# A hybrid decoder layer on one core: retention's state sums in the bank of pv, its normalisation on ScalarE, and the first half of w_out split by casting and adding DMAs

## The chip, the cores and the metric

One of the eight cores of a Trainium2 chip runs the kernel; the others stand idle. The metric is the device time of one execution in microseconds (us); lower is better. The kernel before was timed three times, and one more execution was profiled.

## The reference, cut to what matters

One decoder layer over 512 tokens of width 1024, all in float32:

```
h    = rms_norm(x);  proj = h @ w_in                    # columns split among the head groups
mix  = concat[retention(rq, rk, rv, rg), nsa(...)] @ w_out
x    = x + rms_norm(mix)
x    = x + rms_norm(conv_ffn(rms_norm(x)))
```

Retention has 4 heads and works in chunks of 128 tokens. For each chunk and head:

```
scores  = (q @ k.T) * decay                  # 128 x 128, causal
o       = scores @ v + (q @ state) * xi      # state: 64 x 128, from the chunks before
state   = state * gamma**128 + (k * zeta).T @ v
o       = (o - mean(o)) * rsqrt(var(o) + 1e-5)   # over the 128 columns of the head
y_ret   = silu(g) * (o * gn_w)
```

`mix` is the product of `concat[y_ret, y_nsa]` (512 x 1024) with `w_out` (1024 x 1024).

## The kernel before, in words

Every float32 product is made of three passes over float32r parts: a matrix is split into a high part (`wh`, `xh`, `yh`) and a low part (`wl`, `xl`, `yl`), and `mm3` multiplies high by high, high by low and low by high. So each weight has to be split before TensorE (PE) can take it. There are two ways. `nextw` (through `loadw` and `splitw`) loads the raw weight with a DMA of SyncE (SP), copies it to `wh` on ScalarE (ACT) and subtracts on VectorE (DVE). `castw` lets GpSimd's (POOL's) DMA queue do it:

```
loaded[0] = pool.dma_start(wh, src)                  # casts to float32r while it copies
copy(wl, f(wh), scale=-1.0)                          # on ScalarE
pool.dma_start(wl, src, accum_op=ALU.add)            # adds the source to -wh
```

A class `_Plan` records all operations with a rank, and then sets the order of every engine by itself (`schedule`): it plays the kernel through with its own table of costs, and gives each engine, among the operations that could start within 20 ns of the first, the one of lowest rank. The engines then run their lists in order. The order is fixed at build time. Tiles come from pools by tag, each tag with a number of buffers; a tile takes the next free buffer of its tag in the order in which the program names the tiles.

The stretch that the change touches lies between the attention branches (rank 10) and the output projection (rank 20):

- `ret_a(t)`, for the chunks t = 0 to 3 (rank 5, so ahead of all else): scores `rs` on PE, the mask `sT` on DVE, the output `ro` on PE (with the state `ST` for t > 0), the state's sums `kv` on PE, `ST` brought up to date on DVE, mean and variance of `ro` on DVE (`bs`, `mv`), the reciprocal root `rs` on POOL (a power, and a product with `xi`), and the normalised output into `RV` on DVE. `rs`, `ro` and `kv` are PSUM banks of the tag `m` (`mps`), which has three; the attention's `pv` has a tag of its own with one bank (`pvps`).
- The projection `w_rg` (a `Chunk` of rank 17.8, split by `castw`) gives the gate: `G` and `th` on ACT from four banks `acc`, then products on DVE. Its matmuls (`acc<-wh,xh` and so on, 128x512) stand on PE between those of attention and retention wherever the planner found a gap.
- `ret_b(t)` multiplies `G` by `RV`, transposes it on PE (`tp<-cn,G`, four 128x128 each) and splits it into `yh`, `yl`.
- `c0`, the `Chunk` for the first 512 columns of `w_out` (rank 20): its four weight parts are `wo`, split by `nextw`; parts 0 and 1 take the attention's half of y, parts 2 and 3 retention's. The second 512 columns (`wo1`, banks named `wo`) and the feed-forward follow.

Before a part of rank 0 or 20 is split, line 595 asks `if 0 < plan.rank < 20` for `castw`. All instructions carry line 398, the emitter's, so groups are told apart by tiles.

Of the kernel before, what the change touches and what calls it, by code (L numbers as in the profile page):

```python
# [11 lines left out]
AF = mybir.ActivationFunctionType  # L12
ALU = mybir.AluOpType
AX = mybir.AxisListType

P = 128
# [386 lines left out]
def _body(ctx, tc, io, out, soff, coff):  # L403
# [5 lines left out]
    plan = _Plan(nc)  # L409
    pe, act, dve, pool, sync = (plan.engine(e) for e in (PE, ACT, DVE, POOL, SP))  # L410
# [5 lines left out]
    def nm(s):  # L416
        cnt[0] += 1
        return f"{s}_{cnt[0]}"
# [10 lines left out]
    def k8(shape, dt=F32, n="k"):  # L429
        return plan.tile(gp, shape, dt, nm(n), "k8", 5)  # L430
# [4 lines left out]
    def f2(shape, dt=F32, n="t"):  # L435
        return plan.tile(gp, shape, dt, nm(n), "f2", 6)
# [7 lines left out]
    def tiny(shape, n="y"):  # L444
        return plan.tile(gp, shape, F32, nm(n), "tiny", 16)
# [44 lines left out]
    def castw(src, a, b, wide=False, spare=False):  # L490

        if wide:
            both = k8([P, 2, a, b], F32R, "wb")
            wh, wl = both[:, 0], both[:, 1]
        elif spare:
            wh, wl = (plan.tile(st, [P, a, b], F32R, nm(n), "raw", 2) for n in ("wh", "wl"))
        else:
            wh, wl = (plan.tile(st, [P, a, b], F32R, nm(n), n, 4) for n in ("wh", "wl"))
        loaded[0] = pool.dma_start(wh, src)
        copy(wl, f(wh), scale=-1.0)  # L500
        pool.dma_start(wl, src, accum_op=ALU.add)
        return wh, wl
# [7 lines left out]
    def nextw(src, a, b, eng=dve_pool, **k):  # L510
        return splitw(loadw(src, a, b, **k), eng=eng)
# [35 lines left out]
    def C(name):  # L547
        o, n = coff[name]
        return cn[:, o:o + n]
# [10 lines left out]
    def rsqrt(o, var, n):  # L560
        pool.tensor_tensor(o, var, mhalf[:, :n], op=ALU.pow)
# [21 lines left out]
    def mm3(o, ah, al, bh, bl, start, stop, **k):  # L583
        pe.matmul(o, ah, bh, start=start, stop=False, **k)
        pe.matmul(o, ah, bl, start=False, stop=False, **k)
        pe.matmul(o, al, bh, start=False, stop=stop, **k)

    class Chunk:
# [3 lines left out]
            self.acc = [acc() for _ in range(NT)]  # L592

        def part(self, js, pre=None):
            if 0 < plan.rank < 20 and js[0] >= self.first:
                W = {j: castw(self.src[j], 2, self.n, spare=j == 0) for j in js}
            else:
                W = {j: pre or nextw(self.src[j], 2, self.n, eng=dve if plan.rank else dve_pool) for j in js}
            if 3 in js:
                order = [(j, a, t) for t in range(NT) for j in js for a in range(2)]  # L600
            else:
                order = [(j, a, t) for j in js for a in range(2) for t in range(NT)]
            for j, a, t in order:
                wh, wl = W[j]
                ts = slice(t * P, (t + 1) * P)
                mm3(self.acc[t][:, :self.n], self.lh[j][:, a, ts], self.ll[j][:, a, ts], wh[:, a, :], wl[:, a, :],
                    j == 0 and a == 0, j == 3 and a == 1)
                if j == 3 and a == 1:
                    self.evac(t, self.acc[t])
# [364 lines left out]
    RB = mps  # L974
# [4 lines left out]
    def ret_a(t):  # L979
        rq, rk, rv = RQ[0][:, t], RK[0][:, t], RV[0][:, t, :]  # L980
        m = RB("rs").rearrange("p (h i) -> p h i", h=4)
        for h in range(4):
            pe.matmul(m[:, h, :], rk[:, h // 2, h % 2, :], rq[:, h // 2, :], start=True, stop=True)
        sT = f2([P, 4, P], n="sT")
        dve.tensor_tensor(sT, m, C("rmask").unsqueeze(1).to_broadcast([P, 4, P]), op=ALU.mult)
        o = RB("ro").rearrange("p (h e) -> p h e", h=4)
        for h in range(4):
            pe.matmul(o[:, h, :], sT[:, h, :], rv[:, h * P:(h + 1) * P], start=True, stop=t == 0)
            if t > 0:
                pe.matmul(o[:, h, :], rq[:, h // 2, :], ST[:, h // 2, h % 2, :], start=False, stop=True)  # L990
        if t < 3:
            kvp = RB("kv").rearrange("p (a b e) -> p a b e", a=2, b=2)
            for p in range(2):
                pe.matmul(kvp[:, p].rearrange("p b e -> p (b e)"), RN[0][:, t, p * P:(p + 1) * P],
                          rv[:, 256 * p:256 * p + 256], start=True, stop=True)
            for q in range(2):
                r = slice(64 * q, 64 * q + 64)
                if t > 0:
                    dve.tensor_tensor(ST[r, :, q, :], kvp[r, :, q, :], ST[r, :, q, :], op=ALU.add)
                else:  # L1000
                    dve.tensor_copy(ST[r, :, q, :], kvp[r, :, q, :])
            for p in range(2):
                dve.tensor_scalar(ST[:, p], ST[:, p], gC[:, p:p + 1], None, op0=ALU.mult)
        bs, mv = tiny([P, 4, 6], "bs"), tiny([P, 4, 2], "mv")
        for h in range(4):
            dve.bn_stats(bs[:, h, :], o[:, h, :])
            dve.bn_aggr(mv[:, h, :], bs[:, h, :])
        rs = tiny([P, 4], "rs")
        dve.tensor_tensor(rs, mv[:, :, 1], C("xi2"), op=ALU.mult)
        dve.tensor_scalar(rs, rs, 1e-5, None, op0=ALU.add)  # L1010
        rsqrt(rs, rs, 4)
        pool.tensor_tensor(rs, rs, C("xi"), op=ALU.mult)
        yn = rv.rearrange("p (h e) -> p h e", h=4)
        for h in range(4):
            dve.tensor_scalar(yn[:, h, :], o[:, h, :], mv[:, h, 0:1], rs[:, h:h + 1], op0=ALU.subtract, op1=ALU.mult)

    def ret_b(t):
        ts = slice(t * P, (t + 1) * P)
# [93 lines left out]
    for t in range(NT):  # L1112
        ret_a(t)
# [168 lines left out]
    def prep(a11, a12, s1, s3, w):  # L1282
        s24 = blk(st, "wl", 4, F32)
        b2, b4 = s24[:, 0], s24[:, 1]
        dve.tensor_tensor(b2, s1, a11, op=ALU.subtract)
        for n, src, tag in (("1", a11, "wh"), ("2", a12, "wh"), ("6", b2, "wh"), ("5", s1, "wh"), ("7", s3, "wl"), ("3", b4, "wl")):
            if n == "6":
                dve.tensor_tensor(b4, a12, b2, op=ALU.subtract)
            w[n] = blk(st, tag, 4)
            part(w[n], src)  # L1290
        return w
# [49 lines left out]
    for n, src in (("5", [t13[0]]), ("6", hb[0]), ("7", [t13[1]]), ("4", hb[1])):  # L1341
# [4 lines left out]
        h, l = MV[n]  # L1346
# [104 lines left out]
    for tt in range(2):  # L1451
        b = k8([P, 4, 512], n="base")
# [37 lines left out]
    for j in range(NP):  # L1490
        if j + 2 < NP:
            lasts.append(t_last(j + 2))
        t = plan.tile(st, [P, 2, 512], F32R, nm("t"), ("wh", "wl")[j % 2], 4)
# [59 lines left out]
```

## Time and profile before

| | |
|---|---|
| median of 3 runs | 635.27 us (635.21 to 636.09) |
| the profiled execution | 637.12 us, of which the span from the first to the last instruction is 635.2 us |
| TensorE clock granted, mean | 0.993 of full speed |
| busy share of the span | PE 97%, DVE 86%, ACT 68%, POOL 28% |
| DMA | 100.21 MB, 158 GB/s over the span |

The profile gives busy time for each engine, the waits that ended idle time, and a list of instructions in order of time. An instruction's row has its start, its length, and in brackets the idle time of its engine before it with what released it. A matmul's length overlaps the next one's, so how fast a run of matmuls goes is read from the distance of the starts.

### The profile page before, as it was taken

The numbers are of one execution on the slowest core, as the hardware profiler recorded it, in microseconds if no ns is written. First come the engines' busy times: TensorE is split into PE (matmuls) and PEld (weight loads), VectorE is DVE, ScalarE is ACT, GpSimd is POOL, SyncE is SP. The second block draws the span as 40 slices with busy tenths as digits, with TensorE's granted clock in tenths as the row PEclk, the third lists the DMA queues.
The fourth block names the chain that finished last, engine by engine and source line by source line (L and its number), as shares of the span: only waits on it lengthen the run. The fifth ranks groups of instructions, "written<-read, shape, count | busy, mean of one in ns | idle before, by whom it ended". The sixth has DMA issues, their size and how long they took to land. (4 is left out here: it accounts for less than half of the span.)

```text
span 635.2 us, 10860 instructions
## 1 busy us (share of the span) xinstructions
PE 613.9 (97%) x3781; PEld 542.4 (85%) x3781; DVE 547.1 (86%) x1159; ACT 430.0 (68%) x882; POOL 179.1 (28%) x205
## 2 busy tenths in 40 slices
PE   8998999989999989999999999999999999999996
PEld 5887988878878877889999999999999997787874
DVE  6369876998878899488999998999999999898994
ACT  6667566868997732466867766776777677777761
POOL 0253432433212415024032423233232212231040
PEclk8999999999999999999999999999999999999999
DMA  8762448512412322439359678978967668998452
GB/s 288 267 229 85 151 128 171 133 34 74 94 33 87 114 94 107 162 136 227 80 126 210 141 186 176 201 144 209 196 164 169 150 183 208 224 254 242 140 208 84
DMA packets 41527, 100.21 MB, mean 158 GB/s; under 512 B 4736, under 2 KB 4864, under 8 KB 41472
## 3 DMA queue, kind: packets, MB, share of 16 engines
q0 software_dynamic: 17424, 36.97, 31.0%
q1 hardware_dynamic: 23904, 62.29, 28.4%
q8 instruction: 30, 0.49, 0.3%
q10 hardware_dynamic: 144, 0.26, 0.1%
q14 instruction: 25, 0.20, 0.1%
HBM read 95.30 MB, written 4.19 MB: 157 GB/s over the span
## 5 line engine op out<-in xcount | busy, mean ns | idle before, releaser
L398 POOL DMA_DIRECT2D b<-wup x80 | 63.6, 940 | 152.8 <-ACT b L398 71.9
L398 DVE TENSOR_TENSOR b<-b,b 128x512 fp32r<-128x512 f32 (+1 forms) x160 | 103.8, 683 | 2.7 <-ACT b L398 1.5
L398 ACT ACTIVATE b<-b 128x512 fp32r<-128x512 f32 (+1 forms) x160 | 92.6, 624 | 15.1 <-DMA b<-wup 6.8
L398 PE MATMUL acc<-wl,xh 128*128 128x512 f32 (+1 forms) x192 | 74.5, 388 | 0.2 <-DVE wl L398 0.2
L398 PE MATMUL acc<-wh,xh 128*128 128x512 f32 (+1 forms) x192 | 72.8, 384 | 1.7 <-DVE wh L398 1.7
L398 ACT ACTIVATE wh<-raw 128x1024 fp32r<-128x1024 f32 (+2 forms) x51 | 52.0, 1020 | 32.5 <-PE acc L398 9.4
L398 PE MATMUL acc<-wh,xl 128*128 128x512 f32 (+1 forms) x192 | 73.6, 383 | 0.0
L398 DVE TENSOR_TENSOR wl<-raw,wh 128x1024 fp32r<-128x1024 f32 (+2 forms) x52 | 61.5, 1189 | 7.0 <-ACT wh L398 6.8
L398 PE MATMUL G<-h2h,b 128*128 128x256 f32 x320 | 64.7, 284 | 1.7 <-ACT p L398 1.1
L398 PE MATMUL X<-T,b 128*128 128x256 f32 x480 | 64.9, 284 | 0.6 <-DVE b L398 0.6
L398 PEld LDWEIGHTS X<-T,b 128*128 128x128 f32 x480 | 60.5, 192 | 1.3 <-DVE b L398 1.0
L398 PE MATMUL X<-h2h,b 128*128 128x256 f32 x320 | 61.3, 284 | 0.0
L398 PEld LDWEIGHTS G<-h2h,b 128*128 128x128 f32 x320 | 52.8, 192 | 2.3 <-ACT p L398 1.3
L398 PEld LDWEIGHTS X<-h2h,b 128*128 128x128 f32 x320 | 51.4, 192 | 0.4 <-DVE X L398 0.2
L398 PE MATMUL G<-h2l,b 128*128 128x256 f32 x160 | 45.3, 283 | 0.0
L398 PE MATMUL X<-h2l,b 128*128 128x256 f32 x160 | 45.3, 283 | 0.0
L398 PEld LDWEIGHTS acc<-wh,xh 128*128 128x128 f32 x192 | 36.4, 191 | 7.5 <-ACT xh L398 2.2
L398 PEld LDWEIGHTS acc<-wl,xh 128*128 128x128 f32 x192 | 37.0, 193 | 5.9 <-DVE wl L398 0.7
L398 PEld LDWEIGHTS acc<-wh,xl 128*128 128x128 f32 x192 | 37.0, 193 | 5.4
L398 ACT ACTIVATE P<-P,nmx 128x256 f32<-128x256 f32 (+3 forms) x64 | 35.2, 553 | 4.7 <-DVE nmx L398 4.7
L398 PE MATMUL d<-wl,ah 128*128 128x512 f32 x88 | 34.5, 395 | 0.9 <-DVE wl L398 0.8
L398 PE MATMUL d<-wh,ah 128*128 128x512 f32 x88 | 33.1, 395 | 1.6 <-ACT wh L398 1.6
(291 smaller groups left out, 1640.9 us busy)
## 6 DMA issues: line engine op xcount, KB each, us to landing
b<-wup POOLq DMA_DIRECT2D x80, 256.0 KB, 5.9
b<-wup SPq DMA_DIRECT2D x60, 256.0 KB, 5.8
raw<-wdn SPq DMA_DIRECT2D x19, 512.0 KB, 5.1
T<-wdn POOLq DMA_DIRECT2D x21, 256.0 KB, 5.6
raw<-wo SPq DMA_DIRECT2D x8, 512.0 KB, 3.3
T<-wdn SPq DMA_DIRECT2D x10, 256.0 KB, 5.5
xraw<-xT SPq DMA_DIRECT2D x8, 256.0 KB, 5.4
xnat<-x SPq DMA_DIRECT2D x4, 512.0 KB, 6.2
```

The source lines that it names most:

```text
L398: i = getattr(getattr(self.nc, op.eng), method)(*a, **k)
```

## The change

Three edits. `castw` is also taken at rank 20, so the four weight parts of `c0` are split by POOL's DMAs and ACT rather than by SP's DMAs, ACT and DVE. The state's sums `kv` of chunks 1 and 2 take the bank of `pv` in place of one of the three of `m`. And the normalised output is one ACT instruction per head, `ro * rs + nb`, where DVE makes `nb = -mean * rs` first.

```
-            if 0 < plan.rank < 20 and js[0] >= self.first:
+            if 0 < plan.rank <= 20 and js[0] >= self.first:
                 W = {j: castw(self.src[j], 2, self.n, spare=j == 0) for j in js}
...
-            kvp = RB("kv").rearrange("p (a b e) -> p a b e", a=2, b=2)
+            kvp = (RB if t == 0 else pvps)("kv").rearrange("p (a b e) -> p a b e", a=2, b=2)
...
         yn = rv.rearrange("p (h e) -> p h e", h=4)
+        nb = tiny([P, 4], "nb")
+        dve.scalar_tensor_tensor(nb, mv[:, :, 0], -1.0, rs, op0=ALU.mult, op1=ALU.mult)
         for h in range(4):
-            dve.tensor_scalar(yn[:, h, :], o[:, h, :], mv[:, h, 0:1], rs[:, h:h + 1], op0=ALU.subtract, op1=ALU.mult)
+            act.activation(yn[:, h, :], o[:, h, :], AF.Identity, scale=rs[:, h:h + 1], bias=nb[:, h:h + 1])
```

The planner then sets another order from the end of attention to the first rows of the second half of `w_out`; before and behind that stretch the lists are the same. Numbers of buffers differ between the two builds.

On PE, around the output of chunk 2 (`ro_640` before, `ro_642` now; `acc` with `xh` is the projection `w_rg`). Before:

```order
L398 MATMUL kv_634<-RV_253,RN_254 128x256 x2
L398 MATMUL rs_638<-RQ_251,RK_252 128x128 x4
L398 MATMUL acc_662<-wl_670,xh_127 128x512
L398 MATMUL acc_662<-wh_669,xl_128 128x512
L398 MATMUL acc_662<-wh_669,xh_127 128x512
L398 MATMUL acc_662<-wl_670,xh_127 128x512
L398 MATMUL acc_662<-wh_669,xl_128 128x512
L398 MATMUL ro_640<-RV_253,sT_639 128x128
L398 MATMUL ro_640<-ST_95,RQ_251 128x128
```

Now:

```order
L398 MATMUL kv_635<-RV_253,RN_254 128x256 x2
L398 MATMUL rs_640<-RQ_251,RK_252 128x128 x4
L398 MATMUL acc_664<-wh_673,xh_127 128x512
L398 MATMUL acc_664<-wl_674,xh_127 128x512
L398 MATMUL kv_643<-RV_253,RN_254 128x256 x2
L398 MATMUL acc_664<-wh_673,xl_128 128x512
L398 MATMUL acc_664<-wh_673,xh_127 128x512
L398 MATMUL ro_642<-RV_253,sT_641 128x128
L398 MATMUL ro_642<-ST_95,RQ_251 128x128
```

Before, these were the last five products of `w_rg`; now they are products 7 to 10 of the 24 of its last part, and the state's sums of chunk 2 stand ahead of its output instead of behind it. In all, 15 products of `w_rg`'s last part stood ahead of the first `ro` before, and none stands there now.

On POOL, from the last factors of attention (`cb`) to the reciprocal root of chunk 1 (`rs_637` before, `rs_638` now). Before:

```order
L398 TENSOR_TENSOR cb_572<-ch_570,cn_73 128x512
L398 TENSOR_TENSOR cb_573<-cl_571,cn_73 128x512
L398 TENSOR_TENSOR rs_630<-rs_630,mhalf_69 128x4
L398 TENSOR_TENSOR rs_630<-rs_630,cn_73 128x4
L398 TENSOR_TENSOR rs_637<-rs_637,mhalf_69 128x4
L398 TENSOR_TENSOR rs_637<-rs_637,cn_73 128x4
```

Now:

```order
L398 DMA wh_692<-wo 128x1024
L398 TENSOR_TENSOR cb_572<-ch_570,cn_73 128x512
L398 TENSOR_TENSOR cb_573<-cl_571,cn_73 128x512
L398 DMA wl_693<-wo 128x1024
L398 DMA wh_694<-wo 128x1024
L398 TENSOR_TENSOR rs_630<-rs_630,mhalf_69 128x4
L398 TENSOR_TENSOR rs_630<-rs_630,cn_73 128x4
L398 TENSOR_TENSOR rs_638<-rs_638,mhalf_69 128x4
L398 DMA wl_695<-wo 128x1024
L398 TENSOR_TENSOR rs_638<-rs_638,cn_73 128x4
```

Four of the eight new DMA issues stand among these, one of them between the two steps of chunk 1's reciprocal root; the other four stand earlier, among attention's work.

On ACT, from the last steps of attention to the gate (`G`, `th`). Before:

```order
L398 ACTIVATE wh_691<-raw_690 128x1024
L398 ACTIVATE G_255<-acc_659,hrstd_78 128x512
L398 ACTIVATE G_255<-acc_660,hrstd_78 128x512
L398 ACTIVATE ch_570<-ct_569 128x128
L398 ACTIVATE ph_575<-tp_574 128x512
L398 ACTIVATE pvl_577<-pv_565 64x512
L398 ACTIVATE G_255<-acc_661,hrstd_78 128x512
L398 ACTIVATE yh_653<-y_28_94 128x2x128
L398 ACTIVATE G_255<-acc_662,hrstd_78 128x512
L398 ACTIVATE wh_694<-raw_693 128x1024
L398 ACTIVATE th_671<-acc_659,hrstd_78 128x512
```

Now:

```order
L398 ACTIVATE wl_693<-wh_692 128x1024
L398 ACTIVATE ph_575<-tp_574 128x512
L398 ACTIVATE pvl_577<-pv_565 64x512
L398 ACTIVATE G_255<-acc_663,hrstd_78 128x512
L398 ACTIVATE yh_657<-y_28_94 128x2x128
L398 ACTIVATE RV_253<-ro_626,nb_631,rs_630 128x128 x4
L398 ACTIVATE wl_695<-wh_694 128x1024
L398 ACTIVATE RV_253<-ro_634,nb_639,rs_638 128x128 x4
L398 ACTIVATE G_255<-acc_664,hrstd_78 128x512
L398 ACTIVATE th_675<-acc_663,hrstd_78 128x512
```

The `RV` of chunks 0 and 1 are new here, the copies `wh<-raw` have become `wl<-wh`, and three of the four steps `G` have moved behind them.

## Rows read from the trace of the kernel before

**Rows 1.** The page's first two parts: busy us, share and instructions of each engine over the span, and PE's granted clock in 40 equal slices, in tenths of full speed.
```profile
PE 613.9 (97%) x3781; PEld 542.4 (85%) x3781; DVE 547.1 (86%) x1159; ACT 430.0 (68%) x882; POOL 179.1 (28%) x205
PEclk8999999999999999999999999999999999999999
```
**Rows 2.** Busy time of each engine by stretches (us from the span's start), with granted clock, DMA share and GB/s. Retention runs from 220.87 to about 250.
```profile
core 0: us, PE busy (x) PEld busy (x) DVE busy (x) ACT busy (x) POOL busy (x), PEclk, DMA share, GB/s
150.00:185.00 35.00, 34.97 (x191) 27.84 (x190) 27.29 (x82) 32.35 (x76) 9.37 (x10) 1.00 0.35 76
185.00:200.00 15.00, 15.00 (x85) 12.36 (x84) 13.48 (x58) 13.06 (x41) 3.26 (x3) 1.00 0.23 69
200.00:220.87 20.87, 20.80 (x108) 16.81 (x108) 17.29 (x62) 16.30 (x45) 6.07 (x9) 1.00 0.29 102
220.87:250.00 29.13, 26.28 (x157) 21.80 (x157) 26.99 (x87) 8.24 (x15) 11.86 (x11) 1.00 0.32 110
250.00:262.00 12.00, 11.98 (x57) 9.70 (x56) 8.58 (x16) 4.91 (x11) 0.00 (x0) 1.00 0.27 87
```
**Rows 3.** PE's instructions in retention, in order of time: start, length, instruction, in brackets the idle time before it and its releaser.
```profile
220.87 1.07 PE L398 MATMUL ro<-RV,sT 128*128 128x128 f32 x8
221.78 1.03 PE L398 MATMUL kv<-RV,RN 128*128 128x256 f32 x4
222.65 0.38 PE L398 MATMUL rs<-RQ,RK 128*128 128x128 f32 x2
...
225.39 0.49 PE L398 MATMUL ro<-RV,sT 128*128 128x128 f32 x2
...
227.28 1.03 PE L398 MATMUL kv<-RV,RN 128*128 128x256 f32 x4
228.42 1.16 PE L398 MATMUL rs<-RQ,RK 128*128 128x128 f32 x8
...
231.53 0.49 PE L398 MATMUL ro<-RV,sT 128*128 128x128 f32 x2 [0.79 <-DVE sT L398]
...
235.44 1.16 PE L398 MATMUL rs<-RQ,RK 128*128 128x128 f32 x8 [0.99 <-DVE RV L398]
...
243.01 0.39 PE L398 MATMUL acc<-wh,yl 128*128 128x512 f32 x1
...
245.05 0.39 PE L398 MATMUL acc<-wh,yl 128*128 128x512 f32 x1
246.38 0.63 PE L398 MATMUL tp<-cn,G 128*128 128x128 f32 x4 [0.95 <-DVE G L398]
246.77 0.47 PE L398 MATMUL acc<-wh,yh 128*128 128x512 f32 x1
```
**Rows 4.** DVE's instructions in retention, in order of time, the same columns.
```profile
221.98 0.49 DVE L398 BATCH_NORM_STATS2 bs<-ro 128x6 f32<-128x128 f32 x2 [0.29 <-PE ro L398]
...
224.64 0.69 DVE L398 TENSOR_TENSOR sT<-rs,cn 128x512 f32<-128x512 f32 x1
...
230.81 0.66 DVE L398 TENSOR_TENSOR sT<-rs,cn 128x512 f32<-128x512 f32 x1
...
232.44 1.23 DVE L398 TENSOR_TENSOR wl<-raw,wh 128x1024 fp32r<-128x1024 f32 x1 [0.48 <-ACT wh L398]
...
234.03 1.35 DVE L398 TENSOR_SCALAR RV<-ro,mv,rs 128x128 f32<-128x128 f32 x4
...
243.61 1.36 DVE L398 TENSOR_SCALAR RV<-ro,mv,rs 128x128 f32<-128x128 f32 x4
...
245.55 0.68 DVE L398 TENSOR_TENSOR G<-G,RV 128x512 f32<-128x512 f32 x1
```
**Rows 5.** POOL's instructions from the last factors of attention to the last reciprocal root, in order of time, the same columns.
```profile
209.29 1.43 POOL L398 TENSOR_TENSOR yl<-y,yh 128x256 fp32r<-128x256 f32 x2
...
225.49 1.04 POOL L398 TENSOR_TENSOR rs<-rs,mhalf 128x4 f32<-128x4 f32 x1 [3.58 <-DVE rs L398]
226.61 0.20 POOL L398 TENSOR_TENSOR rs<-rs,cn 128x4 f32<-128x4 f32 x1
...
245.12 3.79 POOL L398 TENSOR_TENSOR rs<-rs,mhalf 128x4 f32<-128x4 f32 x1 [1.45 <-DVE rs L398]
```
**Rows 6.** Groups of instructions over the whole span with their shapes kept apart: operation, out<-in, shapes, count, busy us, mean ns of one, idle time before them. DVE first, then ACT.
```profile
L398 DVE TENSOR_TENSOR wl<-raw,wh 128x1024 fp32r<-128x1024 f32 x46 | 57.0, 1239 | 7.0 <-ACT wh L398 6.8
L398 DVE SCALAR_TENSOR_TENSOR rr<-sums,igates 128x4 f32<-128x4 f32 x24 | 3.7, 157 | 4.0 <-ACT P L398 4.0
L398 ACT ACTIVATE wl<-wh 128x1024 fp32r<-128x1024 f32 x10 | 10.3, 1052 | 1.0 <-DMA wh<-w_rqk 1.0
L398 ACT ACTIVATE ch<-ct 128x128 fp32r<-128x128 f32 x8 | 2.2, 273 | 6.9 <-PE ct L398 6.8
L398 ACT ACTIVATE ph<-tp 128x512 fp32r<-128x512 f32 x40 | 23.1, 589 | 0.9 <-PE tp L398 0.6
L398 ACT ACTIVATE G<-acc,hrstd 128x512 f32<-128x512 f32 x4 | 2.8, 689 | 5.6 <-PE acc L398 5.5
```
**Rows 7.** ACT in order of time: four of its instructions of 128x128 in a run, and the last factor of attention.
```profile
212.74 1.28 ACT L398 ACTIVATE P<-P,rr 128x128 f32<-128x128 f32 x4 [0.17 <-DVE rr L398]
...
219.52 0.27 ACT L398 ACTIVATE ch<-ct 128x128 fp32r<-128x128 f32 x1
```
**Rows 8.** DMA issues: destination, source, queue, count, KB each, median us from issue to landing.
```profile
raw<-wo SPq DMA_DIRECT2D x8, 512.0 KB, 3.3
wh<-w_rg POOLq DMA_DIRECT2D x4, 512.0 KB, 3.7
wl<-w_rg POOLq DMA_DIRECT2D x4, 512.0 KB, 5.2
wh<-w_rqk POOLq DMA_DIRECT2D x2, 512.0 KB, 4.1
wl<-w_rqk POOLq DMA_DIRECT2D x2, 512.0 KB, 9.1
```
**Rows 9.** What touches `w_rg`: POOL's time for an issue in ns (least, median, most), with the first and last start.
```profile
L398 POOL DMA_DIRECT2D wh<-w_rg x4: 547/577/777, 121.7 to 162.0; - x4
L398 POOL DMA_DIRECT2D wl<-w_rg x4: 874/885/908, 135.4 to 178.0; - x4
```

## Prediction

> **What bounds the kernel.** I read the page's busy shares first: PE is busy for 613.9 of 635.2 us at a granted clock of 0.9 or more in every slice but the first [rows 1]. So a change is worth only what it takes out of PE's idle time, or puts in. The busy time by stretches says where that lies near the change: attention, 150 to 220.87 us, leaves PE idle for 0.10 us in all, and the output projection behind 250 us for 0.02; but retention, 220.87 to 250, has PE busy for 26.28 of 29.13 us, an idle 2.85 us. In the same stretch DVE is busy for 26.99 us and ACT for 8.24 [rows 2]. PE's own rows name the waits: 0.79 us before the third `ro` (for the mask `sT`), 0.99 before the last `rs` (for `RV`, which had not yet left its bank) and 0.95 before the first transpose of `G`; with 2.73 us they are nearly all of it [rows 3]. All three end on DVE. The rows of DVE show why: the mask of 230.81 came behind other work, `RV` at 234.03 behind a weight split of 1.23 us, and `G` at 245.55 behind another four `RV` [rows 4]. The clock stays at 1.00 from 150 us on [rows 2], so nothing is to be had there.
>
> **The change part by part.** The matmuls stay the same; only their order changes, between the last units of attention and the first rows of the second half of w_out.
>
> *w_out by casting DMAs.* Four subtractions leave DVE, 4 x 1.24 = 5.0 us [rows 6], two or so of them in attention, two in retention. On ACT each copy `wh<-raw` becomes a copy `wl<-wh` of the same size, 1.05 us [rows 6]: nothing. SP loses four issues. POOL gains four casting and four adding ones, 4 x 0.58 + 4 x 0.89 = 5.9 us [rows 9]; it is busy for 11.86 of 29.13 us in retention and 6.07 of 20.87 before it [rows 2], so this lies in gaps, except where a POOL result is waited for behind an issue (below). The adding DMA reads the weight a second time, 2 MB more in all; the DMA share there is 0.23 to 0.32 [rows 2]. Landing takes 3.7 and 5.2 us in place of 3.3 [rows 8].
>
> *Normalisation on ACT.* Sixteen DVE instructions go, four runs of 1.36 us [rows 4], 5.4 us; four of 0.16 (`nb`, like `rr`, [rows 6]) come. On ACT an instruction of 128x128 out of PSUM takes 273 ns, and an operand of one column per partition adds 100 (689 against 589 at 512 columns) [rows 6], so two make it about 473; four of 392 in a run took 1.28 us [rows 7], 0.30 apart, 0.09 less than one alone, so I take 4 x 0.38 + 0.09 = 1.6 us. The sixteen are 6.4 us on an engine that has 20.9 us to spare. The bounds for the four: 1.3 (rows 7's run, one operand) and 1.9 (four of 473 without overlap). The Trainium skill, ScalarE: Activation LUTs, section Rules for kernel authors, says to do adds and products on VectorE, not on ScalarE. By that rule the 5.4 us would stay on DVE; the chain below would keep 1.4 us a chunk, and of the waits perhaps the 0.99 alone would go, 634.3 us. The rows speak for the move: the engine with less to do is ACT.
>
> *The bank.* `rs`, `ro`, `kv` share three banks. A `ro` frees its bank only after statistics, POOL's root and `RV`; with `kv` elsewhere from chunk 1 on, two banks alternate for `ro` and one serves the `rs`, so no `rs` waits for the `RV` of an earlier chunk.
>
> *What is late next.* I walk PE's new order with the durations of [rows 3] and set 0 at the first `ro`: it takes 0.91, a `kv` 0.87, an `rs` about 0.85, a later `ro` 1.89 (225.39 to 227.28), a product 0.227 (nine between 243.01 and 245.05). DVE follows the first `ro` as before: statistics to the mask of the next chunk, 221.98 to 225.33, takes 3.35 us [rows 4].
> - `ro` of chunk 1: PE is there at 4.45 (0.91 + 0.87 + 0.85 and eight products), its mask is done at 4.46 (225.33 minus 220.87). At most 0.1 lost.
> - Reciprocal root of chunk 0: POOL ends at 5.9 (226.81, [rows 5]); `nb` 6.2, `RV` on ACT 6.3 to 7.9, then ACT's `wl` copy to 9.0. Its source was issued at about 1, lands at about 5.
> - `ro` of chunk 2: DVE starts the statistics at 6.3 rather than behind `RV`; mask at 9.6; PE is there at 9.85.
> - Root of chunk 1: the power 9.8 to 10.85, then the adding DMA's issue, 0.89, then the factor 0.2: 12.0. This is the added wait: DVE stands at `nb` of chunk 1 from 10.65 to 12.0, and the statistics and mask of chunk 3 behind it end at 14.55; PE asks for that mask at 14.87. The cover is 0.3 us. `RV` on ACT ends at 13.9 and frees the bank that this `ro` may need.
> - Transposes: PE gets to the first at 22.0 (23 products behind the last `ro`). PE ends the last product of the gate at 17.7, ACT needs 0.69 each for its `th` and `G` [rows 6], so 19.1, and DVE ends the first `G<-G,RV` four steps of about 0.65 later (0.68 in [rows 4]): 21.7. A group of transposes holds PE for 0.39 (246.38 to 246.77). The third transpose: PE 25.7, DVE 25.4. The fourth: PE 29.4; the last root starts at 25.6, 1.04 for the power, 0.2, `nb`, 1.6 for `RV`, 0.65 for `G`: 29.6.
>
> So what stays is four places where data and PE arrive within 0.3 us of each other. A handover took 0.06 us (`sT` at 230.81 plus 0.66, `ro` at 231.53) and 0.15 (`G` at 245.55 plus 0.68, `tp` at 246.38) [rows 3, 4]. I put 0.1 on the first, 0.2 on the first transpose, 0.1 on the third, 0.35 on the fourth: 0.75 us come back. **Sum:** -2.85 + 0.75 = -2.1 us. Attention I leave at nothing: PE has 0.07 us of idle there now, and work moves off DVE. 15 products (3.4 us) move from attention to retention; their cover goes, and that is the second rival's and the third's ground. The profiled execution took 637.12 us, 1.92 outside its span, 1.85 above the median of 635.27; -2.1 gives 635.0 for one like it and **633.2 us** for a median.
>
> **The rivals.**
> - *A, the forecast:* the three waits go, 0 to 1.6 us come back: 632.4 to 634.0.
> - *B, the waits move to the tail.* POOL's power took 1.04 us, but 3.79 while DVE ran products of two SBUF operands [rows 5]. Between the third and the fourth transpose PE has 15 products and no slack; if the last power takes 3.79 there, 2.75 us are added to the fourth transpose: -2.1 + 2.75 = +0.65, 635.9; with half of that, 634.5. For it: the same instruction, the same gate work nearby. Against it: in the new order DVE's steps beside the last power read a PSUM operand (`yl<-tp`), as beside the power that took 1.04, and the SBUF products stand before it.
> - *C, slower: ACT stands behind a late casting DMA.* `wh` of part 2 can be issued at about 211.3 (209.29 plus 1.43 plus 0.58, [rows 5, 9]). ACT's copy of it stands ahead of attention's last `ph`, and is reached at about 216.8: the last `ch` at 219.52 [rows 7] less 3.4 for the 15 products, plus two short steps. So 5.5 us are free; each us beyond holds up ACT, the `ph`, and PE in its order. A landing of 3.7 or 4.1 [rows 8] costs nothing; 9.1, the median of an adding one in `w_rqk`, costs 3.6: -2.1 + 3.6 = +1.5, 636.8; from 8.9 on the kernel is slower by over 0.2%. The Trainium skill, DMA: Bandwidth & Descriptors, section SWDGE vs HWDGE vs iDMA, says that GpSimd writes these descriptors into SBUF, in a state from which VectorE locks it out in one of its modes, and that SyncE's DMAs are immune; no row of these issues shows it, at 547 to 908 ns each [rows 9].
> - *D, the edit does not do what it says* (the planner puts the work back on DVE or keeps a late order). The order rules out the first: the sixteen instructions are on ACT.
>
> **How the numbers follow.** A change of 0.2%, 1.27 us, is about the least that a measurement of this kernel can tell. A gets 0.66, all of it faster but a strip near 634.0: 0.62 faster, 0.04 the same. B 0.25: nearly all within 0.2% (634.0 to 636.5), 0.22, with 0.02 faster and 0.01 slower. C 0.07, 0.06 of it slower. D or a mixture 0.02, the same. Faster 0.64, same 0.29, slower 0.07. The range starts at 632.3 (all of 2.85 and a little of the runs' own spread) and ends at 635.4, which leaves out the worst of B, and C.
>
> **What would show it.** Right: PE idle below 1.2 us from its first `ro` to the fourth transpose, that first `ro` at about 217.5 us, no wait of PE for `RV` or `sT` above 0.3, DVE in that stretch some 7 us lighter and ACT some 6 heavier, four runs `RV<-ro` of about 1.6 us on ACT, and the rest of the kernel shifted by 2 us without change. B would show as one wait of over 1 us at a transpose, with POOL's power above 2 us. C would show as ACT's idle time ended by a DMA `wh<-wo`, and a PE wait for `ph` or `pl`. The prediction is wrong if PE loses its time in attention, or somewhere behind 250 us where raw weights of the second half now load later because the spare buffers are held.

## The result, and the profile after

The changed kernel took **630.06 us** in the median of four runs (629.68 to 632.38), the kernel before 635.68 beside it (635.21 to 637.33): ratio 0.9927, 95% interval 0.9903 to 0.995. The forecast was 633.2 us with a range of 632.3 to 635.4. The sign held, and so did most of the mechanism; the gain was larger than the range allowed. Three later comparisons of the same kernel gave ratios of 0.9959 (0.9925 to 0.9993), 0.9971 (0.9945 to 0.9997) and 0.9935 (0.991 to 0.9961). All four intervals hold 0.9945 to 0.995, a gain of about 3.3 us; the first comparison lay at the lucky end.

The page's busy times and granted clock, as [rows 1]:

```profile
PE 612.3 (98%) x3781; PEld 542.8 (86%) x3781; DVE 536.3 (85%) x1145; ACT 436.2 (69%) x898; POOL 178.6 (28%) x211
PEclk9999999999999999999999999999999999999998
```

DVE lost 10.8 us and ACT gained 6.2. By stretches, as [rows 2]; retention now runs from 214.53 to about 243.5:

```profile
193.00:214.53 21.53, 21.53 (x120) 18.07 (x119) 18.21 (x88) 17.96 (x59) 10.22 (x13) 1.00 0.50 118
214.53:243.50 28.97, 28.97 (x174) 24.94 (x173) 22.11 (x79) 14.30 (x33) 7.16 (x11) 1.00 0.47 121
243.50:256.00 12.50, 12.50 (x59) 10.34 (x58) 7.42 (x11) 6.95 (x15) 0.00 (x0) 1.00 0.61 226
```

PE is busy for all of retention, where it had been idle for 2.85 us. PE's rows show no wait in brackets, as against the three of [rows 3]: the first `ro` of each chunk, the product ahead of the first transpose, and the four transposes of `G`:

```profile
214.53 1.05 PE L398 MATMUL ro<-RV,sT 128*128 128x128 f32 x8
...
219.03 0.49 PE L398 MATMUL ro<-RV,sT 128*128 128x128 f32 x2
...
224.62 0.46 PE L398 MATMUL ro<-RV,sT 128*128 128x128 f32 x2
...
229.69 0.45 PE L398 MATMUL ro<-RV,sT 128*128 128x128 f32 x2
...
236.56 0.39 PE L398 MATMUL acc<-wh,yh 128*128 128x512 f32 x1
236.80 0.60 PE L398 MATMUL tp<-cn,G 128*128 128x128 f32 x4
...
239.56 0.60 PE L398 MATMUL tp<-cn,G 128*128 128x128 f32 x4
...
240.69 0.60 PE L398 MATMUL tp<-cn,G 128*128 128x128 f32 x4
...
244.56 0.60 PE L398 MATMUL tp<-cn,G 128*128 128x128 f32 x4
```

What they take comes from DVE, the three masks and then `G` (compare [rows 4]):

```profile
218.28 0.69 DVE L398 TENSOR_TENSOR sT<-rs,cn 128x512 f32<-128x512 f32 x1
...
223.78 0.69 DVE L398 TENSOR_TENSOR sT<-rs,cn 128x512 f32<-128x512 f32 x1
...
228.88 0.65 DVE L398 TENSOR_TENSOR sT<-rs,cn 128x512 f32<-128x512 f32 x1
...
235.79 1.28 DVE L398 TENSOR_TENSOR G<-G,RV 128x512 f32<-128x512 f32 x2
...
239.30 0.69 DVE L398 TENSOR_TENSOR G<-G,RV 128x512 f32<-128x512 f32 x1 [0.55 <-ACT RV L398]
...
243.55 0.69 DVE L398 TENSOR_TENSOR G<-G,RV 128x512 f32<-128x512 f32 x1 [1.24 <-ACT RV L398]
```

The masks end at 218.97, 224.47 and 229.53, 0.06, 0.15 and 0.16 us before the `ro` that reads them. The third `G` ends 0.70 before its transpose and the fourth (243.55 plus 0.69) 0.32 before its own. On ACT the four `RV` of a chunk take 1.50 us; further down two rows that decide a later step:

```profile
220.84 1.50 ACT L398 ACTIVATE RV<-ro,nb,rs 128x128 f32<-128x128 f32 x4 [0.58 <-DVE nb L398]
...
242.01 1.50 ACT L398 ACTIVATE RV<-ro,nb,rs 128x128 f32<-128x128 f32 x4 [0.29 <-DVE nb L398]
...
261.70 0.63 ACT L398 ACTIVATE w<-raw 128x512 fp32r<-128x512 f32 x1 [1.67 <-DMA raw<-wup]
262.24 0.58 ACT L398 ACTIVATE junk<-wo 128x512 bf16<-128x512 f32 x1
```

POOL's powers for the last two chunks (one 1.56 us, beside DVE's products of two SBUF operands, the last 1.01) and the landings of the new DMAs, as [rows 5] and [rows 8]:

```profile
230.10 1.56 POOL L398 TENSOR_TENSOR rs<-rs,mhalf 128x4 f32<-128x4 f32 x1 [3.37 <-DVE rs L398]
...
240.15 1.01 POOL L398 TENSOR_TENSOR rs<-rs,mhalf 128x4 f32<-128x4 f32 x1 [8.11 <-DVE rs L398]
```
```profile
wh<-wo POOLq DMA_DIRECT2D x4, 512.0 KB, 5.1
wl<-wo POOLq DMA_DIRECT2D x4, 512.0 KB, 5.8
```

**Three stretches.** To compare executions I read three starts on PE: the first `cs<-KC` (the last attention unit), the first `wo<-wh,yh` (second half of `w_out`) and the first `up<-h2h,wh` (feed-forward). Up to the first the two kernels' instructions and their order are the same; on PE they differ from 180 to 277 us of the kernel before, so also behind the first `wo`, as far as the transposes of `xres` ahead of the first `up`. Times in us, one profiled execution each, two of before and four of the changed kernel:

| execution | front: start to `cs` | middle: `cs` to `wo` | behind: `wo` to `up` |
|---|---|---|---|
| before | 166.98 | 96.50 | 23.67 |
| before, again (ctl_before) | 165.14 | 96.52 | 23.83 |
| changed | 163.82 | 92.34 | 24.02 |
| changed (ctl_change) | 168.94 | 92.29 | 24.68 |
| changed (change_again) | 166.33 | 92.31 | 25.43 |
| changed (change_beside) | 164.94 | 92.35 | 24.58 |

The middle gains 4.2 us each time, to 0.06. The front varies by 5 us over the six, on code that is the same up to there. Behind, the changed kernel gives back 0.3 to 1.7 us. From the first `up` to the end the lists are the same again: 348.0 and 347.4 us before, 347.7, 348.2, 347.3 and once 352.3 in the changed kernel, which is spread. So the gain is 4.2 less about 0.9 (the mean of 24.02, 24.68, 25.43 and 24.58 less that of 23.67 and 23.83), 3.3 us, in keeping with the four intervals.

### The profile page after: what moved, and what is told of

Its sections match the earlier page's. It is cut to its first block, busy times and chain, and to the rows that moved or that the text cites. A ratio compares the mean times of both kernels' runs of the same rounds, so it can differ in the third digit from the quotient of the medians.

```text
span 627.9 us, 10872 instructions
## 1 busy us (share of the span) xinstructions
PE 612.3 (98%) x3781; PEld 542.8 (86%) x3781; DVE 536.3 (85%) x1145; ACT 436.2 (69%) x898; POOL 178.6 (28%) x211
## 5 line engine op out<-in xcount | busy, mean ns | idle before, releaser
L398 DVE TENSOR_TENSOR wl<-raw,wh 128x1024 fp32r<-128x1024 f32 (+2 forms) x48 | 56.5, 1184 | 9.4 <-ACT wh L398 9.2
L398 ACT ACTIVATE wh<-raw 128x1024 fp32r<-128x1024 f32 (+2 forms) x47 | 47.7, 1016 | 22.8 <-issue 6.9
```

The lines of the kernel that those rows point to most:

```text
L398: i = getattr(getattr(self.nc, op.eng), method)(*a, **k)
```

## The experiments

Ratios are to the kernel before on the same chip, with 95% intervals.

**Is the gain in the middle, and is the front chance?** Both kernels again, and two of the edits alone:

```
only_cast:  if 0 < plan.rank <= 20 and js[0] >= self.first:      (nothing else changed)
only_act:   nb = -mean * rs on DVE; act.activation(yn, o, AF.Identity, scale=rs, bias=nb)
```

> The kernel before once more, unchanged. Two stretches are read: the front, from the start to the first product cs<-KC of attention (167.0 us in the trace of before, 163.8 in that of the change, in lists that are the same instruction for instruction up to there), and the middle, from there to the first product of the second half of w_out (96.5 us before, 92.4 in the change). Theory 1 (the change gives 4.1 us, all in the middle; the 3.2 us in front are chance of one execution, above all a race of DVE and POOL at 134.8 us, where three DVE instructions took 3.09 us instead of 1.07): the front comes out anywhere between 163.5 and 167, and the middle at 96.5 within 0.3. Theory 2 (the change gives the 3.2 us in front too, by something that the order does not show): the front is 167.0 within 0.3 again.

> The changed kernel once more. Theory 1: the front lies anywhere between 163.5 and 167, the middle at 92.4 within 0.3; over five rounds the change gives 4 to 5 us. Theory 2: the front is 163.8 within 0.3 again, and over five rounds the change gives over 6 us.

> The first edit alone: w_out's first half by casting and adding DMAs, kv in its old bank, the normalisation on DVE. Theory 1 (it is the load of DVE that makes PE wait): the weight splits leave DVE, but the 5.4 us of RV stay, so the wait for RV before a score product stays near 1 us and the middle is 94 to 95.5 us. Rival (the bank makes it): the same wait of 1 us and the middle at 95.5 to 96.5. The lists behind the middle are reordered as well, so the whole time can differ by some us for reasons of its own; the verdict is read from the middle.

> The third edit alone: the normalisation on ACT, kv in its old bank, w_out's first half still split on DVE. Theory 1: RV no longer waits behind the weight splits of DVE nor holds up the masks, so the waits for RV and sT go, one before the transposes stays; the middle is 93 to 94.5 us. Rival (the casting DMAs give most, since they free DVE in attention too): the middle stays above 95. Again only the middle is read.

Measured: the kernel before 1.0001 (0.9973 to 1.0029), with the stretches of the table. The changed kernel 0.9959, a gain of 2.6 us where 4 to 5 were expected; its front, 168.94, was the longest of all and beyond the expected 167, so the first execution's short front was chance. The casting DMAs alone: middle 94.43, ratio 0.9978 (0.9953 to 1.0003), one wait of 0.81 left before the first transpose. Normalisation on ACT alone: 93.43, 0.9939 (0.9908 to 0.9971), one wait of 0.73 left before the third `ro`. PE's row for each:

```profile
240.20 0.63 PE L398 MATMUL tp<-cn,G 128*128 128x128 f32 x4 [0.81 <-DVE G L398]
```
```profile
230.84 0.49 PE L398 MATMUL ro<-RV,sT 128*128 128x128 f32 x2 [0.73 <-DVE sT L398]
```

Theory 1 holds for the amounts: both middles lie in its ranges. Which wait stays it had wrong both times: with the casting DMAs the wait for `RV` went and one for `G` stayed, with normalisation on ACT the waits at the transposes went and one for `sT` stayed.

**What is the bank worth?** The rest of the combinations, built from the same three edits (kv in `RB` or in `pvps`, line 992, and the two above):

> The first and the third edit without the bank (kv stays in m). 'Middle' is the time from PE's first cs to its first wo product of the second half; it took 96.50 and 96.52 us in the two profiles of the kernel before, 92.34 and 92.29 in the two of the changed kernel, 94.43 with the first edit alone, 93.43 with the third alone. Theory 1 (the loss is PE waiting for VectorE's masks, RV and G; an edit is worth the VectorE work that it takes out; the bank is worth nothing by itself): 92.2 to 92.8. Theory 2 (the bank lets rs and kv go ahead of an RV that still holds its bank, and the sum of 4.2 needs it): 93.0 or more, with a wait of PE of over 0.5 us before an rs or ro.

> The second and the third edit without the casting DMAs. Theory 1: the middle as with the third alone (93.43), 93.1 to 93.7, and the wait of 0.73 before the third ro may stay, since VectorE's order there still holds the weight splits. Theory 2: 92.3 to 92.9.

> The second edit alone. Theory 1: VectorE has the same work, so PE's waits stay or move: middle 95.8 to 97.0. Theory 2: the wait of 0.99 before the last rs goes (it waited for the bank of an RV) and does not come back: 95.3 or less.

> The first and second edit, normalisation left on VectorE. So far the middle (PE's first cs to its first wo product) is 96.5 with none of the edits, 94.4 with the first alone, 94.9 with the bank alone, 93.4 with the third alone, 92.2 with the first and third, 94.5 with the second and third, 92.3 with all. If the edits' savings added up, 96.5 - 2.1 - 1.6 = 92.8. If what counts is whether data is there when the planner has placed PE's step (the theory now): the three last transposes still wait for VectorE's four RV (1.36 us a chunk), a wait for G of some 0.5 to 1 us stays, and the middle is 93.3 to 94.6.

| edits | middle, us | ratio (95%) |
|---|---|---|
| none | 96.50, 96.52 | |
| bank | 94.91 | 0.998 (0.9958 to 1.0002) |
| cast | 94.43 | 0.9978 (0.9953 to 1.0003) |
| cast, bank | 93.92 | 0.9991 (0.9968 to 1.0015) |
| act | 93.43 | 0.9939 (0.9908 to 0.9971) |
| act, bank | 94.53 | 0.9978 (0.9946 to 1.001) |
| cast, act | 92.23, 92.35 | 0.9924 (0.9892 to 0.9956), 0.9961 (0.9941 to 0.998) |
| all three | 92.29 to 92.35 | 0.9927 to 0.9971 |

Neither theory got the bank right throughout. Alone it is worth 1.6 us, as theory 2 had it (the waits of 0.79 and 0.99 are gone, 0.29 before the last `ro` and 0.94 before the first transpose are left), with the casting DMAs 0.5 (within the range of the second theory, but with waits of 0.25 for `ST` and 0.28 for `sT` in place of the expected one for `G`), with both other edits nothing, and with normalisation on ACT it costs 1.1. PE's wait there (`act, bank`), and DVE's mask that it waited for:

```profile
231.44 0.48 PE L398 MATMUL acc<-wh,xl 128*128 128x512 f32 x1
233.77 0.46 PE L398 MATMUL ro<-RV,sT 128*128 128x128 f32 x2 [1.85 <-DVE mv L398]
```
```profile
232.97 0.66 DVE L398 TENSOR_TENSOR sT<-rs,cn 128x512 f32<-128x512 f32 x1
```

The releaser named is `mv`, but it is the mask, done at 233.63, that the `ro` at 233.77 reads. In that order one product stands between the `rs` and the `ro` of the last chunk; with the third edit alone there were eight, and the mask was covered. So the savings don't add up: each edit changes the planner's order, and what counts, as this pair and the next test suggest, is whether products stand where data is late.

**The same pair again, and a late root.** The last one does POOL's power of chunk 3 three times (its values are then other ones, so only its times are of use):

```
+        for _ in range(3 if t == 3 else 1):
             rsqrt(rs, rs, 4)
```

> The changed kernel once more, beside the version without the bank. Middle 92.2 to 92.4, front (start to PE's first cs) anywhere from 163.8 to 169; ratio to before 0.990 to 0.996.

> First and third edit, no bank. If the bank is worth nothing beside the other two, the same as the changed kernel in the same job: medians within 1.2 us of each other, intervals overlapping, middle 92.1 to 92.4. If the bank brings something elsewhere: slower than the changed kernel by over 1.5 us.

> The changed kernel with GpSimd's power of the last chunk done three times in place of once (the values of that chunk are other ones): the last root comes some 2.1 us later. The planner moves only the fourth transpose of G back behind 15 more products of the output projection. In the forecast each place where data and PE come together within 0.3 us was charged 0.1 to 0.35 us. Theory (the planner keeps every such place covered by products for as long as it has any, and PE loses nothing there): middle 92.2 to 92.7, no wait of PE above 0.3 us. Rival (slack is lost): 0.3 us of it is used up and PE waits 1.0 to 1.8 us at that transpose: middle 93.3 to 94.1.

Measured: 0.9971 and 0.9961 with overlapping intervals, so the bank is worth nothing measurable beside the other two. The late root: middle 92.34 with no wait in it, ratio 0.995 (0.9923 to 0.9977). Its power, its `G` and its fourth transpose (first on POOL, then DVE, then PE):

```profile
242.83 3.18 POOL L398 TENSOR_TENSOR rs<-rs,mhalf 128x4 f32<-128x4 f32 x3 [8.12 <-DVE rs L398]
```
```profile
250.10 0.69 DVE L398 TENSOR_TENSOR G<-G,RV 128x512 f32<-128x512 f32 x1 [0.17 <-ACT RV L398]
```
```profile
250.82 0.39 PE L398 MATMUL acc<-wh,yh 128*128 128x512 f32 x1
251.05 0.60 PE L398 MATMUL tp<-cn,G 128*128 128x128 f32 x4
```

2.1 us more on the chain cost nothing: the planner put 17 more products ahead of the transpose (32 behind the third one, 15 in the changed kernel, where 15 more were expected), and PE came 0.26 us behind the data. That a place has only 0.3 us in hand is no loss by itself. The planner knew of this delay when it set the order; a delay that it doesn't foresee is not tested here.

**The front.** One source of its spread is a meeting of DVE and POOL, here in the kernel before, which lost, and in the changed kernel, which won; DVE and POOL of the one, its PE behind them, then of the other:

```profile
134.81 3.09 DVE L398 TENSOR_SCALAR P<-P,rr 128x384 f32<-128x384 f32 x3
```
```profile
135.99 1.70 POOL L398 TENSOR_TENSOR rb<-xr,cn 128x256 f32<-128x256 f32 x2
```
```profile
138.75 0.50 PE L398 MATMUL pv<-pl,VV 128*128 128x512 f32 x1 [1.51 <-DVE pl L398]
```
```profile
133.62 1.07 DVE L398 TENSOR_SCALAR P<-P,rr 128x384 f32<-128x384 f32 x3
```
```profile
134.83 1.69 POOL L398 TENSOR_TENSOR rb<-xr,cn 128x256 f32<-128x256 f32 x2
```

Three DVE products take 3.09 us or 1.07, with the same order and with POOL's `rb` 1.18 or 1.21 us behind their start. In the first the third product alone took 2.43 us, and ended 0.21 after `rb`. In 16 profiles with `rb` on POOL this meeting was lost in 6, whichever edits they had. From PE's first `s` product to the first `cs` the ten others took 65.8 to 65.9 us and these six 67.7 to 67.8, so about 1.9 us of the front's spread are this. I moved the rotary products of that chunk to DVE (line 953):

```
-        rope(xr, xr, 8, t, split=(qn, kn), eng=dve_pool)
+        rope(xr, xr, 8, t, split=(qn, kn), eng=dve if t == 2 else dve_pool)
```

> The changed kernel, with chunk 2's rotary products on VectorE instead of partly on GpSimd, so that no GpSimd product rb stands beside VectorE's three P<-P,rr of 128x384. Race theory (these three take 3.1 us when GpSimd's rb gets in first, 1.07 when not, and PE then waits 1.5 us before pv<-pl; three of six profiles show it): no P<-P,rr group above 1.5 us there, no wait of PE above 0.5 us near 138 us; front (PE's first cs) 163.5 to 167 us; the median some 0.5 to 1.5 us below the changed kernel's 632.6 of the last comparison, ratio to before about 0.993 to 0.996. Rival (the loss comes from VectorE's load there, not from GpSimd): VectorE has some 1.4 us more to do, a wait for pl of 1 us or more stays near 138 to 141 us, and the ratio is 0.996 or above.

Measured: the three products took 1.08 us, PE's wait near 138 was gone, and the ratio was 0.9953 (0.9933 to 0.9972), no better than the changed kernel's. One profile doesn't show that POOL's `rb` is the cause, since ten of 16 were free of the loss with it; that goes by the six rows alone, in all of which the third product ends some 0.2 us behind `rb`. From PE's first `s` product to the first `wo` it took 159.46 us, against 158.11 in the changed kernel when the meeting was won and 160.05 in ctl_change, where it was lost: the edit takes back most of what the meeting costs. Its middle was 94.51 us in place of 92.3, in another order of the planner's; one wait of 0.43 for DVE's `y` is in it, and where the rest goes was not traced.

**What is given back behind 250 us?** In the changed order ACT's copy of a feed-forward weight (`w<-raw`, from `wup`) stands ahead of the row sum of the first `wo` bank (`junk<-wo`). Both in change_again, and what PE then waits for:

```profile
265.60 0.63 ACT L398 ACTIVATE w<-raw 128x512 fp32r<-128x512 f32 x1 [3.24 <-DMA raw<-wup]
266.14 0.58 ACT L398 ACTIVATE junk<-wo 128x512 bf16<-128x512 f32 x1
```
```profile
272.76 0.66 PE L398 MATMUL tp<-cn,xres 128*128 128x128 f32 x4 [1.49 <-DVE xres L398]
```

In the kernel before the row sum stood first:

```profile
269.17 0.60 ACT L398 ACTIVATE junk<-wo 128x512 bf16<-128x512 f32 x1 [3.08 <-PE wo L398]
```

It started 5.69 us behind the first `wo` product (263.48) there, 7.50 (258.64) in change_again. The load that this copy waits for was not issued later than before: 1.2 us behind the first `wo` in all four profiles of the changed kernel, 2.05 in the two of the kernel before. It landed 5.52 to 6.93 us behind the first `wo`, before 6.27 and 6.81. But now the copy starts 0.02 or 0.03 us after the landing and the row sum half a us after that, and `wo` to `up` follows: 24.02 us with the landing at 5.52, 24.58 at 6.07, 24.68 at 6.18 and 25.43 at 6.93. The same order comes with the casting DMAs alone (24.16) and with the bank added (24.90); the versions without them took 23.66 to 23.83.

The test tells the planner that the loads land later:

```
+    plan.late = 1000        # 2000 in cast_act_wup_late
     ws = [rows(io["wup"][0, 0], KT, P), rows2(io["wup"][0, 1], KT, P, pt),
           ...
+    plan.late = 0
```

> The changed kernel, with the planner told that the four loads of the feed-forward's first weights land 1 us later; it then sets ScalarE's row sum of the first wo bank ahead of the copy w from raw, and the first transposes of xres three products later. Middle unchanged, 92.2 to 92.4. If the wait for that DMA ahead of the row sum is what gives time back: row sum 5.6 to 5.8 us behind the first wo product (6.1 to 7.5 in the changed kernel), no wait of PE for tp from xres above 0.3 us, first wo to first up 23.5 to 23.9 us, and a median about 1 us below that of the changed kernel beside it. If it is something else, such as the DMAs themselves or the longer chain behind them: 24.0 us or more with a wait still there.

> Casting DMAs and normalisation on ScalarE without the bank, and the planner told that the four loads land 2 us later, so that VectorE's mix and ScalarE's first xres square no longer stand behind the copies and subtractions of w. Middle 92.1 to 92.4; first wo to first up 23.5 to 23.9 in place of 23.66 and 24.80 in two profiles of that version. If the theory holds, the fastest version so far: ratio to before 0.989 to 0.995.

> The changed kernel beside these two. Middle 92.2 to 92.4; row sum 6.0 to 7.6 us behind the first wo product, first wo to first up 24.0 to 25.5; ratio to before 0.992 to 0.997.

Measured in change_wup_late, whose first `wo` is at 257.65:

```profile
263.35 0.60 ACT L398 ACTIVATE junk<-wo 128x512 bf16<-128x512 f32 x1 [1.82 <-PE wo L398]
...
264.38 1.15 ACT L398 ACTIVATE w<-raw 128x512 fp32r<-128x512 f32 x2 [0.34 <-DMA raw<-wup]
```

The row sum is 5.70 behind, no wait of PE is left, and `wo` to `up` takes 23.69 us (23.70 in the other version), against 24.58 in the changed kernel beside it: the place of the loss is shown. The first transposes of `xres` moved too, behind 59 products of the second half and not 55. It isn't the only way to lose there. Without the bank the row sum stands first even without this test, 5.70 behind, and one profile took 23.66 us but the other (cast_act_again) 24.80, with the load's landing at 6.31 and 7.78, and with this wait:

```profile
272.00 0.66 PE L398 MATMUL tp<-cn,xres 128*128 128x128 f32 x4 [0.84 <-DVE xres L398]
```

The times do not resolve it: 0.995 (0.9924 to 0.9977) and, without the bank, 0.9928 (0.9897 to 0.9959), against 0.9935 (0.991 to 0.9961). The expected further gain of about 1 us in the median was not seen, and no version here is measurably faster than the changed kernel.

## Why the prediction was wrong in size

- *The waits to be taken out.* "An idle 2.85 us" was too small a reading. Idle time in brackets is counted from the modelled end of the matmul before, and a product's row is 0.39 long where the next starts after 0.227. By starts, the first transpose of [rows 3] came 1.33 us after the product before it, at 245.05: 1.10 lost, not 0.95. In the same way the third `ro` lost 0.95 and the `rs` at 235.44 lost 1.17; `rs` at 228.42 lost 0.28 and the fourth transpose 0.19 with nothing in brackets. That makes 3.69 us in five places. The other 0.5 of the 4.2 lies in pieces below 0.25 us each, part of it in attention, and is not assigned. PE's rows of the kernel before that this needs beside [rows 3]:

```profile
230.35 0.39 PE L398 MATMUL acc<-wh,xl 128*128 128x512 f32 x1
...
233.41 1.03 PE L398 MATMUL kv<-RV,RN 128*128 128x256 f32 x4
...
251.42 0.40 PE L398 MATMUL acc<-wl,yh 128*128 128x512 f32 x1
251.84 0.66 PE L398 MATMUL tp<-cn,G 128*128 128x128 f32 x4
```

- *"0.75 come back": a charge without a ground.* Next to nothing came back in the middle: PE's rows show no wait, and by starts one slip of 0.14 is left, before the third `ro` (224.25 to 224.62). The walk itself held: counted from the first `ro`, the forecast had PE at the second, third and fourth `ro` at 4.45, 9.85 and 14.87 us and at the first, third and fourth transpose at 22.0, 25.7 and 29.4; measured 4.50, 10.09, 15.16, 22.27, 26.16 and 30.03; what is more there are longer steps, 0.22 to 0.32 us from product to product. But the charges of 0.1 to 0.35 us laid on top were wrong in kind. The handovers of 0.06 and 0.15 us behind them were measured where PE stood waiting, and where products cover the place they cost nothing; the late root shows that 2.1 us more on such a chain cost nothing while the planner knows of them and has products to put there.
- *Behind 250 us.* The forecast left nothing there, and named raw weights that load later as what could make it wrong. Time was lost there, 0.3 to 1.7 us, but the load in question was not issued later: in the changed kernel it is ACT's place for a copy ahead of a row sum.
- *What held.* `RV` on ACT was 1.50 us a chunk (forecast 1.6, bounds 1.3 and 1.9), ACT 6.1 us heavier over retention (forecast 6); the waits for `sT`, `RV` and `G` went. DVE was only 4.9 us lighter there, not 7: one weight split had lain in that stretch and not two (232.44, [rows 4]), and the last `RV` mostly behind it. The first `ro` came 6.3 us earlier, of which 3.2 are the front. Rival B did not happen: the last power took 1.01 us. The late root's 2.1 us more were known to the planner; a power that DVE slows while it runs, as in the rival, was not tried. Rival C did not either: the casting DMAs landed after 5.1 and 5.8 us, later than the 3.7 and 5.2 taken, and no wait of ACT ended on one.
- *The order of the edits' worth.* Normalisation on ACT brings most, 3.1 us of the middle alone. The forecast weighed it against the Trainium skill's rule (ScalarE: Activation LUTs, section Rules for kernel authors) that adds and products belong on VectorE. The 634.3 us that it took from that did not come. The Trainium skill, Perfetto Trace Analysis, section Optimizing Scalar/DVE Operations, has the exception: where VectorE is saturated, moving work to ScalarE may make sense. The traces agree with that page here: the move alone took the middle from 96.5 to 93.4.

Taken together, by the traces: -4.2 in the middle where the forecast had -2.85 and +0.75, and +0.9 behind where it had nothing, -3.3 us; forecast -2.1. The 5.6 of the first comparison has 2 us or so of chance in it, of which the front is the part that the traces show: of the two first profiles the one before lost the meeting of DVE and POOL and the changed one won it. That part of the miss is luck, and no step of the forecast.

## What to carry to other kernels

Read a pipelined engine's loss from the distance of starts against its usual distance, not from idle time alone, and charge nothing for a place only because data and engine come close, where whoever sets the order knows both times: ask instead what could be placed there if the data came later. In a kernel whose planner sets the order, an edit's worth depends on the edits beside it, so measure combinations; and follow the order far behind the edit, where a copy moved ahead of a short step can wait for a DMA.

## What was unexpected in the hardware

Three DVE products of 128x384 with a per-partition factor took 1.07 or 3.1 us on the same code. In the longer case the third ended 0.21 us after POOL's two `rb` products, as if it had waited out nearly the whole of them. In all six lost profiles `rb` starts 0.51 or 0.52 us behind the start of the third product, in the ten others 0.55 or 0.56: a few hundredths go with 2 us, and which is the cause of the other isn't shown. The Trainium skill, SBUF — State Buffer, section SBUF: two separate sides, says that the port pair which VectorE shares with GpSimd is an exclusive lock: a VectorE instruction that needs it (in a mode with two ports, or with two SBUF inputs) or a GpSimd one holds it for the whole instruction, whichever starts first, and the other is blocked. Whether these products run in such a mode no row shows. The rows agree in that one waits the other out; by the page whoever starts first wins, whereas here the product that lost has a record that starts at 135.47 and POOL's at 135.99.

The front also holds the start of PE's clock. The same window of the changed kernel and of change_no_race (columns as in [rows 2], the granted clock third from the end):

```profile
10.00:15.00 5.00, 5.00 (x23) 4.09 (x22) 4.12 (x6) 4.22 (x6) 0.00 (x0) 1.00 0.94 346
```
```profile
10.00:15.00 5.00, 5.00 (x14) 3.92 (x14) 4.66 (x7) 4.33 (x6) 0.00 (x0) 0.57 0.88 306
```

At 1.00 (2.4 GHz) PE got through 23 matmuls, at a mean of 0.57 (mostly the lower level, 1.2 GHz) through 14. Ahead of it PE was busy for 3.72 of the 5 us from 5 to 10 in the first and 2.02 in the second, waiting for its first weights.

So early in the span the distance of starts has to be read beside the clock column. In ctl_change the same window says 1.00 too, with 15 matmuls:

```profile
10.00:15.00 5.00, 5.00 (x15) 3.95 (x14) 4.64 (x7) 4.09 (x6) 0.00 (x0) 1.00 0.84 287
```

There the products start 0.43 us apart as far as 13.86, as they do at 0.50 in change_no_race, and 0.23 apart behind it; in the changed kernel's first profile they start 0.23 apart from 10.04 on. The first `s` product came at 101.18 and 98.05 us.
